# All block sums on VectorE, and a first pair that begins with products without sums

## The chip, the cores and the metric

The kernel runs on one core of one Trainium2 chip. The core has five engines, each with its own in-order queue: TensorE (PE) for matmuls, with PEld loading its weights beside it, VectorE (DVE), ScalarE (ACT), GpSimd (POOL) and SyncE (SP), which issues most of the DMA transfers. The metric is the device time of one execution in microseconds (us); the median of three runs counts.

## What is computed

One layer of a hybrid decoder on 1024 positions of width 1024: a feed-forward block, a mixer, a second feed-forward block, each behind a norm that a conditioning vector `c` scales and shifts. Cut to the part that the change touches (sh, sc and g come from `silu(c) @ w_ada + b_ada`):

```python
def swiglu(h, w_gate, w_up, w_down):
    return (jax.nn.silu(h @ w_gate) * (h @ w_up)) @ w_down

h = modulate(rmsnorm(x, norm_ffn1[l]), sh1, sc1)
x = x + 0.5 * g1[:, None, :] * swiglu(h, ffn1_w_gate[l], ffn1_w_up[l], ffn1_w_down[l])
h = modulate(rmsnorm(x, norm_mix[l]), sh2, sc2)
x = x + g2[:, None, :] * hybrid_mixer(h, ...)
h = modulate(rmsnorm(x, norm_ffn2[l]), sh3, sc3)
x = x + 0.5 * g3[:, None, :] * swiglu(h, ffn2_w_gate[l], ffn2_w_up[l], ffn2_w_down[l])
```

All is float32; the hidden width of each feed-forward block (FFN1, FFN2) is 2816, that is 22 tile columns of 128.

## The kernel before

**Split products.** Each float32 operand is split into a high part rounded to fp32r (`whi`, `bh`) and a low part, the difference (`wlo`, `bl`). A product is three passes on PE: high by high (line 167 in `mm3`), high weight by low input (line 168), low weight by high input (line 169). A weight tile's split (`parts`) is a cast on ACT (line 158) and a subtraction on DVE (line 159). The loaded weights (`raw`) have four slots, so have `whi` and `wlo`.

**Gate and up.** In each FFN the first two tile columns (the *first tiles*) are plain three-pass products. The other twenty are done in ten pairs. A pair is a 2x2 block product by a scheme of seven products instead of eight (`seven`, lines 384 to 431), once for gate and once for up, 168 matmuls of 128x512 in all. Its order is product 1, 2, 6, 5, 7, 4, 3. Products 1, 2 and 4 take blocks of the input as they are; 3, 5, 6 and 7 take sums of blocks, s4, s1, s2 and s3. Of the weights, products 1, 2 and 3 take loaded blocks, 6 and 5 the sums `ta`, 7 and 4 the sums `tb`.

**The sums.** `blocks` (lines 344 to 363) makes the input sums of an FFN once, behind its first tiles: 16 additions of high and low on POOL (line 354), 16 sums on DVE (lines 355 to 358), then a cast on ACT (line 360) and a subtraction on DVE (line 361) for each. `weight_blocks` (lines 365 to 382) makes four sums for each weight on POOL (line 372), 160 in both FFNs, and splits all seven parts. The weight sums stand in tiles `comb`.

**Around the pairs.** After each product a copy on ACT (line 398) keeps a partial result and additions on DVE (line 394) finish it; silu on ACT and the product of gate and up on DVE (line 486) follow, and POOL stores the result (line 446). In FFN1 `side_work` runs between the pairs: `ada_vec` computes nine slices of the conditioning (512 KB loads, additions on DVE in line 209), and `rope_tables` the position tables (some 46 small DVE operations). Here the scheduler of the tile framework sets the order on each engine; a few places are pinned.

**First tiles.** In FFN1 (`first_tiles`) the first half of the positions has been done during startup; the second half is scaled (line 303), shifted and cast on ACT (line 308) and its low part formed on DVE (line 312), step by step, then the first tiles' second half runs. `act` (line 449) makes silu and product of a tile column. In FFN2 `first_tiles2` does both halves. **Behind the pairs** `hidden` loads the results back as inputs of the down projection, and `down` (line 515) loads the down weights when it first needs them.

Of the kernel before, what the change touches and what calls it, by code (L numbers as in the profile page):

```python
# [15 lines left out]
ALU = mybir.AluOpType  # L16
# [43 lines left out]
ACT0 = (3, 6)  # L60
# [45 lines left out]
class Layer:  # L106
# [25 lines left out]
    def open_weights(self, nraw, nsplit, size):  # L132
        if self.wctx is not None:
            self.wctx.close()
        self.wctx = ExitStack()
        self.ctx.push(self.wctx)
        self.wts = self.wctx.enter_context(self.tc.tile_pool(name="wts", bufs=1, side="right", reuse_waits="tile"))
        self.wraw, self.wsplit, self.wsize = nraw, nsplit, size

# [174 lines left out]
    def ada_norm(self, xT, b, hh, hT, tp, spread=(), order=None, make=None):  # L314
# [3 lines left out]
        if make is not None:  # L318
            hT.append(make())
        for j in range(KT):  # L320
# [23 lines left out]
    def blocks(self, hT, s1, s2, s4, tp):  # L344

        nc = self.nc
        (h0, l0), (h1, l1) = hT
        s3 = (h1[:, 0:4], l1[:, 0:4])
        f = lambda x: x.bitcast(F32)
        for j in range(4):  # L350
            t = {}
            for name, (h, l), k in (("a21", hT[1], j), ("a22", hT[1], j + 4), ("a11", hT[0], j), ("a12", hT[0], j + 4)):
                t[name] = tp.tile([P, 512], F32, name="g", bufs=8)
                nc.gpsimd.tensor_tensor(out=t[name], in0=f(h[:, k]), in1=f(l[:, k]), op=ALU.add)
            nc.vector.tensor_tensor(out=t["a22"], in0=t["a21"], in1=t["a22"], op=ALU.add)
            nc.vector.tensor_tensor(out=t["a21"], in0=t["a11"], in1=t["a21"], op=ALU.subtract)
            nc.vector.tensor_tensor(out=t["a11"], in0=t["a22"], in1=t["a11"], op=ALU.subtract)
            nc.vector.tensor_tensor(out=t["a12"], in0=t["a12"], in1=t["a11"], op=ALU.subtract)
            for name, (hi, lo) in (("a11", s2), ("a22", s1), ("a12", s4), ("a21", s3)):
                nc.scalar.copy(out=hi[:, j], in_=t[name])  # L360
                nc.vector.tensor_tensor(out=lo[:, j], in0=t[name], in1=f(hi[:, j]), op=ALU.subtract)  # L361
        half = lambda p, i: (p[0][:, 4 * i:4 * i + 4], p[1][:, 4 * i:4 * i + 4])
        return {1: half(hT[0], 0), 2: half(hT[0], 1), 3: s4, 4: half(hT[1], 1), 5: s1, 6: s2, 7: s3}

    def weight_blocks(self, w, t):
# [4 lines left out]
        ta, tb = [self.wts.tile([P, 8, P], F32, name="comb", bufs=2) for _ in range(2)]  # L370
        b11, b21, b12, b22 = r1[:, 0:4], r1[:, 4:8], r2[:, 0:4], r2[:, 4:8]
        tt = lambda o, x, y, op: nc.gpsimd.tensor_tensor(out=o, in0=x, in1=y, op=op)  # L372
# [5 lines left out]
        for src, names in ((r1, (1, 2)), (ta, (6, 5)), (tb, (7, 4)), (b22, (3,))):  # L378
            hi, lo = self.parts(src, (4 * len(names), P))
            for i, n in enumerate(names):  # L380
                out[n] = [(hi[:, 4 * i + k], lo[:, 4 * i + k]) for k in range(4)]
        return out

    def seven(self, A, B, new):
# [5 lines left out]
        def product(n, out, first):  # L390
            self.mm3(out, B[n], self.krows(A[n]), first=first, skip=not first)
# [42 lines left out]
    def ffn(self, hT, sums, xd, wg, wu, wd, b, tp, side, begin, mid, quarters, ws):  # L434
# [13 lines left out]
        def act(ps, t, hh):  # L448
            s = self.tmp.tile([P, 512], F32, name="t")
            nc.scalar.activation(out=s, in_=ps[0], func=AF.Silu)  # L450
            a = tp.tile([P, 512], F32, name="g", bufs=8)
            nc.vector.tensor_tensor(out=a, in0=s, in1=ps[1], op=ALU.mult)
# [15 lines left out]
        begin(load, gateup_mm, act, gateup)  # L468
        A = self.blocks(hT, *sums(), tp)
# [45 lines left out]
        def down(c, o, hh, n, c0=0, w=512):  # L515
# [1208 lines left out]
```

## Time and profile before

| what | us |
|---|---|
| median of three runs (lowest, highest) | 2371.13 (2369.62, 2372.92) |
| the profiled execution | 2369.87 |
| its span on the core | 2368.1 |
| PE busy | 2200.5 |
| DVE busy | 1414.8 |
| ACT busy | 877.4 |
| POOL busy | 446.4 |

The profile is one execution; its span is what the engines took, the execution's own time has a little around it. Busy time is the sum of an engine's instructions. PE's is modelled, and a matmul's row is longer than the distance to the next one, so small stops show in the distance only. A line of waits says for whom an engine stood still (the producer that came last), how long in all and how often. FFN1's pairs lie between 107 and 580 us of the span, FFN2's between 1658 and 2085; the mixer is between them.

### The profile page before, as it was taken

How to read it: one execution, taken by the hardware profiler on the slowest of the kernel's cores; microseconds unless marked ns; L12 is line 12 of the kernel's file. 1: busy time of each engine (PE TensorE's matmuls, PEld its weight loads, DVE VectorE, ACT ScalarE, POOL GpSimd, SP SyncE). 2: the span in 40 equal slices, each digit the busy share in tenths (PEclk: the TensorE clock that was granted, in tenths of full speed). 3: DMA queues.
4: the chain of work that ended last, by engine and by line, in shares of the span. 5: the costliest groups of instructions: out<-in, count | busy, mean ns of one | idle time of the engine just before them, and what ended most of it. 6: DMA issues, size and time to landing. Idle time of an engine off the chain costs nothing. (4 is left out here: it accounts for less than half of the span.)

```text
span 2368.1 us, 27357 instructions
## 1 busy us (share of the span) xinstructions
PE 2200.5 (93%) x10431; PEld 1800.2 (76%) x10431; DVE 1414.8 (60%) x2151; ACT 877.4 (37%) x1409; POOL 446.4 (19%) x428
## 2 busy tenths in 40 slices
PE   5859999999999999999999999999599999989997
PEld 4647777777878778877778898887477777768787
DVE  7896775445333664456986888867744444443346
ACT  4232223333112433276534766623333333321133
POOL 4443223331000110000212011102533333200000
PEclk9879999999999999999999999999799999999999
DMA  8124655226233331245554000232022222252234
GB/s 290 37 91 162 195 188 167 81 80 222 62 107 103 108 119 45 64 127 155 188 187 134 16 19 22 90 134 85 22 85 76 85 76 85 76 205 80 98 111 138
DMA packets 113491, 261.36 MB, mean 110 GB/s; under 512 B 10208, under 2 KB 31072, under 8 KB 113360
## 3 DMA queue, kind: packets, MB, share of 16 engines
q1 hardware_dynamic: 97712, 214.85, 28.1%
q0 software_dynamic: 11088, 37.17, 4.3%
q10 hardware_dynamic: 4560, 7.60, 0.9%
q8 instruction: 82, 1.34, 0.2%
q14 instruction: 49, 0.40, 0.1%
HBM read 212.46 MB, written 47.12 MB: 110 GB/s over the span
## 5 line engine op out<-in xcount | busy, mean ns | idle before, releaser
L167 PE MATMUL dn<-bh,whi 128*128 128x512 f32 (+1 forms) x1104 | 426.7, 387 | 19.8 <-ACT whi L158 17.5
L169 PE MATMUL dn<-bh,wlo 128*128 128x512 f32 (+1 forms) x1104 | 425.7, 386 | 3.2 <-DVE wlo L159 1.6
L168 PE MATMUL dn<-bl,whi 128*128 128x512 f32 (+1 forms) x1104 | 425.6, 386 | 2.4 <-DVE bl L306 2.4
L158 ACT CAST whi<-raw 128x1024 fp32r<-128x1024 f32 (+4 forms) x230 | 205.7, 897 | 530.5 <-PE dn L168 253.9
L167 PE MATMUL mm<-bh,whi 128*128 128x512 f32 x880 | 349.6, 398 | 20.0 <-ACT whi L158 8.6
L169 PE MATMUL mm<-bh,wlo 128*128 128x512 f32 x880 | 345.7, 394 | 6.3 <-DVE wlo L159 5.7
L168 PE MATMUL mm<-bl,whi 128*128 128x512 f32 x880 | 344.3, 392 | 0.7 <-DVE bl L361 0.7
L159 DVE TENSOR_TENSOR wlo<-raw,whi 128x1024 fp32r<-128x1024 f32 (+3 forms) x219 | 249.3, 1138 | 128.5 <-ACT whi L158 126.5
L167 PEld LDWEIGHTS dn<-bh,whi 128*128 128x128 f32 x1104 | 211.1, 191 | 63.2 <-ACT whi L158 20.5
L169 PEld LDWEIGHTS dn<-bh,wlo 128*128 128x128 f32 x1104 | 210.9, 191 | 46.4 <-DVE wlo L159 3.9
L168 PEld LDWEIGHTS dn<-bl,whi 128*128 128x128 f32 x1104 | 210.9, 191 | 44.8 <-DVE bl L306 3.3
L159 DVE TENSOR_TENSOR wlo<-comb,whi 128x1024 fp32r<-128x1024 f32 x80 | 98.9, 1238 | 212.0 <-ACT whi L158 209.7
L524 DVE SCALAR_TENSOR_TENSOR x<-dn,gat,x 128x512 f32<-128x512 f32 (+1 forms) x104 | 73.7, 708 | 246.8 <-PE dn L169 246.8
L167 PEld LDWEIGHTS mm<-bh,whi 128*128 128x128 f32 x880 | 165.9, 189 | 60.2 <-DVE t L394 10.7
L169 PEld LDWEIGHTS mm<-bh,wlo 128*128 128x128 f32 x880 | 166.2, 189 | 47.2 <-DVE wlo L159 12.2
L168 PEld LDWEIGHTS mm<-bl,whi 128*128 128x128 f32 x880 | 166.5, 189 | 34.7 <-DVE bl L361 1.0
L158 ACT CAST whi<-comb 128x1024 fp32r<-128x1024 f32 x80 | 84.2, 1053 | 229.9 <-PE mm L168 208.3
L372 POOL TENSOR_TENSOR comb<-raw 128x512 f32<-128x512 f32 x80 | 108.5, 1360 | 263.7 <-DVE wlo L159 170.4
L167 PE MATMUL mm<-x,whi 128*128 128x512 f32 x280 | 112.6, 403 | 32.9 <-ACT g L398 22.1
L169 PE MATMUL mm<-x,wlo 128*128 128x512 f32 x280 | 112.7, 403 | 6.4 <-DVE wlo L159 5.1
L168 PE MATMUL mm<-x,whi 128*128 128x512 f32 x280 | 111.4, 398 | 1.9 <-DVE x L312 1.2
L446 POOL DMA_DIRECT2D a_d<-g x88 | 48.4, 550 | 301.4 <-DVE g L486 253.5
(337 smaller groups left out, 3821.2 us busy)
## 6 DMA issues: line engine op xcount, KB each, us to landing
raw<-w_ada SPq DMA_DIRECT2D x56, 512.0 KB, 4.1
raw<-wg SPq DMA_DIRECT2D x44, 512.0 KB, 3.6
raw<-wu SPq DMA_DIRECT2D x44, 512.0 KB, 3.5
a_d<-g POOLq DMA_DIRECT2D x88, 256.0 KB, 2.5
raw<-a_d SPq DMA_DIRECT2D x44, 512.0 KB, 4.2
raw<-wd SPq DMA_DIRECT2D x32, 512.0 KB, 4.6
raw<-win SPq DMA_DIRECT2D x31, 512.0 KB, 3.5
raw<-wd SPq DMA_DIRECT2D x40, 384.0 KB, 3.2
```

The lines of the kernel that those rows point to most:

```text
L158: self.made = nc.scalar.copy(out=hi, in_=r)
L159: (engine or nc.vector).tensor_tensor(out=lo, in0=r, in1=hi.bitcast(F32), op=ALU.subtract)
L167: nc.tensor.matmul(out=out, lhsT=ah, rhs=bh, start=first and i == 0, stop=False, skip_group_check=skip)
L168: nc.tensor.matmul(out=out, lhsT=ah, rhs=bl, start=False, stop=False, skip_group_check=skip)
L169: nc.tensor.matmul(out=out, lhsT=al, rhs=bh, start=False, stop=last and i == n - 1, skip_group_check=skip)
L372: tt = lambda o, x, y, op: nc.gpsimd.tensor_tensor(out=o, in0=x, in1=y, op=op)
L446: nc.gpsimd.dma_start(out=a_d[t, :, hh * 512:hh * 512 + 512], in_=a)
L524: nc.vector.scalar_tensor_tensor(out=xs, in0=ps[:, 0:w], scalar=self.gat[:, 8 * b + o:8 * b + o + 1], in1=xs, op0=ALU.mult, op1=ALU.add)
```

## The change

All block sums move from POOL to DVE, and the code around them is written in another order:

- `blocks` becomes `second_half`. It scales all eight steps of the second half first, then makes high, shifted value and low of each step, the shifted value on ACT and in place, in the order 0, 4, 1, 5, 2, 6, 3, 7. After the first tiles it makes the other sums, on DVE.
- `weight_blocks` makes its sums on DVE and splits a part only when a product asks for it (`get`).
- The first pair begins with products 1 and 2 of gate and of up. Then come 6, 5, 7 of gate, 6 of up, 4 and 3 of gate, 5 and 7 of up, and 4 and 3 of up in the next pair.
- In FFN1 the first eleven steps of the side work (the slice `ada_vec(2)` and the loads behind it) are issued behind the last block subtraction.
- `act` writes in place; `ACT0`, which put the first half's `act` between two steps, is gone. The first down weights are loaded ahead of the first hidden tiles; in FFN2 the stores of x (`x3_d`) come ahead of the first tiles. The tiles of a weights pool are declared when it is opened.

The diff, cut to its core:

```diff
-    def blocks(self, hT, s1, s2, s4, tp):
+    def second_half(self, x, r, b, hT, s2, rest, tp):
...
+        order = (0, 4, 1, 5, 2, 6, 3, 7)
+        t, u = {}, {}
+        for j in order:
+            t[j] = tp.tile([P, 512], F32, name="g", bufs=8)
+            nc.vector.scalar_tensor_tensor(out=t[j], in0=self.cols(x, j, 512, 512), scalar=self.scl[:, 8 * b + j:8 * b + j + 1],
+                                           in1=r, op0=ALU.mult, op1=ALU.mult)
+        s1, s4 = rest()
         s3 = (h1[:, 0:4], l1[:, 0:4])
-        f = lambda x: x.bitcast(F32)
+        for j in order:
+            shift = self.mod[:, 24 * b + j:24 * b + j + 1]
+            nc.scalar.activation(out=h1[:, j], in_=t[j], func=AF.Identity, bias=shift)
+            nc.scalar.activation(out=t[j], in_=t[j], func=AF.Identity, bias=shift)
+            nc.vector.tensor_tensor(out=l1[:, j], in0=t[j], in1=f(h1[:, j]), op=ALU.subtract)
+
+        yield None
...
+        def split(src, dst, j):
+            nc.scalar.copy(out=dst[0][:, j], in_=src)
+            self.made = tt(dst[1][:, j], src, f(dst[0][:, j]), ALU.subtract)
+
         for j in range(4):
-            t = {}
-            for name, (h, l), k in (("a21", hT[1], j), ("a22", hT[1], j + 4), ("a11", hT[0], j), ("a12", hT[0], j + 4)):
-                t[name] = tp.tile([P, 512], F32, name="g", bufs=8)
-                nc.gpsimd.tensor_tensor(out=t[name], in0=f(h[:, k]), in1=f(l[:, k]), op=ALU.add)
-            nc.vector.tensor_tensor(out=t["a22"], in0=t["a21"], in1=t["a22"], op=ALU.add)
...
+            whole(j)
+            tt(t[j + 4], t[j], t[j + 4], ALU.add)
+            tt(t[j], u[j], t[j], ALU.subtract)
+            tt(u[j], t[j + 4], u[j], ALU.subtract)
+            split(u[j], s2, j)
+            split(t[j + 4], s1, j)
+        for j in range(4):
+            split(t[j], s3, j)
+            whole(j + 4)
+            tt(u[j + 4], u[j + 4], u[j], ALU.subtract)
+            split(u[j + 4], s4, j)
...
     def weight_blocks(self, w, t):
...
-        tt = lambda o, x, y, op: nc.gpsimd.tensor_tensor(out=o, in0=x, in1=y, op=op)
+        tt = lambda o, x, y, op: nc.vector.tensor_tensor(out=o, in0=x, in1=y, op=op)
...
+        def get(n):
+            if n not in out:
+                src, names = next(x for x in ((r1, (1, 2)), (ta, (6, 5)), (tb, (7, 4)), (b22, (3,))) if n in x[1])
+                hi, lo = self.parts(src, (4 * len(names), P))
...
-        begin(load, gateup_mm, act, gateup)
-        A = self.blocks(hT, *sums(), tp)
+        A = begin(load, gateup_mm, act, gateup)
+        made = self.made.ins
...
-            for us in (g, up_units(t, res)):
+            u = up_units(t, res)
+            if t == 2:
+                self.weave(g[:2] + u[:2])
+                if side is not None:
+                    with self.tc.issue_after(made):
+                        for _ in range(11):
+                            next(side)
+                self.weave(g[2:5] + u[2:3] + g[5:] + u[3:5], [side])
+                held = u[5:]
+                continue
+            for us in (g, u):
...
+        weights(0, 0, 8)
         hidden(0, 0, 8)
```

In the changed code the matmul lines are 170 to 172, the weight cast and subtraction 161 and 162, the block sums 377, the weight sums 405, the additions 431, the product of gate and up 522, that of the first tiles 488.

PE at the end of the first pair's gate products 1 and 2 in FFN1, before (`bh_88` and `bl_89` are the input's first half, `x_670` holds sums):

```order
L168 MATMUL mm<-bl_89,whi 128x512
L167 MATMUL mm<-x_670,whi 128x512
L168 MATMUL mm<-x_670,whi 128x512
L169 MATMUL mm<-x_670,wlo 128x512
L167 MATMUL mm<-x_670,whi 128x512
L168 MATMUL mm<-x_670,whi 128x512
```

and now (`bh_92`, `bl_93` the same half, `s_522` the sum s2), at the end of the second of up:

```order
L172 MATMUL dn<-bh_92,wlo 128x512
L170 MATMUL dn<-bh_92,whi 128x512
L171 MATMUL dn<-bl_93,whi 128x512
L172 MATMUL dn<-bh_92,wlo 128x512
L170 MATMUL mm<-s_522,whi 128x512
L171 MATMUL mm<-s_522,whi 128x512
L172 MATMUL mm<-s_522,wlo 128x512
```

Where gate's product 2 ran straight into a product with sums, up's products 1 and 2 now stand before it.

DVE in FFN1's first pair before: the last first-tile products (line 452) and weight splits, then the block sums and subtractions (355 to 361), which wait for POOL:

```order
L159 TENSOR_TENSOR wlo<-raw,whi 128x1024
L452 TENSOR_TENSOR g<-t,dn 128x512
L159 TENSOR_TENSOR wlo<-comb,whi 128x1024 x2
L452 TENSOR_TENSOR g<-t,dn 128x512
L159 TENSOR_TENSOR wlo<-raw,whi 128x512
L355 TENSOR_TENSOR g<-g 128x512
L207 TENSOR_SCALAR t<-raw,cact 128x512
L356 TENSOR_TENSOR g<-g 128x512
```

and now: after the last first-tile product (line 488) come the block sums of line 377, of which the list shows the last ones, and only then the low half of `comb`, that is of ta, for product 6:

```order
L377 TENSOR_TENSOR x_539<-t,x_539 128x512
L377 TENSOR_TENSOR t<-t 128x512
L377 TENSOR_TENSOR t<-bh_92,bl_93 128x512
L431 TENSOR_TENSOR g<-g,dn 128x512
L377 TENSOR_TENSOR x_539<-t,x_539 128x512
L377 TENSOR_TENSOR t<-t 128x512
L431 TENSOR_TENSOR t<-t,dn 128x512
L162 TENSOR_TENSOR wlo<-comb,whi 128x1024
L377 TENSOR_TENSOR x_539<-t,x_539 128x512
L405 TENSOR_TENSOR comb<-raw 128x512
```

The rows between are of the same kind: from the product of line 488 to that subtraction there are 32 operations of 128x512, two of them additions of line 431. In FFN2's first pair the same count stands ahead of the low half of tb, which product 7 needs.

DVE in a late pair of FFN2 before, about the end of gate's product 2 (line 394 is an addition that waits for PE, here `dn` holds product 2):

```order
L394 TENSOR_TENSOR t<-t,mm 128x512
L159 TENSOR_TENSOR wlo<-raw,whi 128x512
L486 TENSOR_TENSOR g<-g,t 128x512
L394 TENSOR_TENSOR g<-g,dn 128x512
L159 TENSOR_TENSOR wlo<-raw,whi 128x1024
L159 TENSOR_TENSOR wlo<-comb,whi 128x1024
```

and now:

```order
L431 TENSOR_TENSOR t<-t,mm 128x512
L162 TENSOR_TENSOR wlo<-raw,whi 128x1024
L522 TENSOR_TENSOR g<-g,t 128x512
L431 TENSOR_TENSOR g<-g,dn 128x512
L162 TENSOR_TENSOR wlo<-raw,whi 128x512
L162 TENSOR_TENSOR wlo<-comb,whi 128x1024
```

The low half of up's loaded blocks (`wlo<-raw,whi 128x1024`), which stood behind the product of line 486 and the addition of gate's product 2, now stands ahead of both. The weight sums of line 405 follow a few rows on.

## Rows read from the trace of the kernel before

**Rows 1.** The page's part 1: busy us (share of the span) xinstructions, by engine.

```profile
PE 2200.5 (93%) x10431; PEld 1800.2 (76%) x10431; DVE 1414.8 (60%) x2151; ACT 877.4 (37%) x1409; POOL 446.4 (19%) x428
```

**Rows 2.** What PE waited for, 100 to 160 us: total us, times, longest.

```profile
PE mm L167 <- ACT g L398: 21.9, 1, 21.9
PE mm L167 <- ACT whi L158: 8.6, 1, 8.6
```

**Rows 3.** The same, 1650 to 1705 us.

```profile
PE mm L167 <- ACT g L398: 17.8, 1, 17.8
PE mm L167 <- ACT whi L158: 7.7, 1, 7.7
```

**Rows 4.** Stretches: length, busy us (xinstructions) by engine, PEclk, DMA share, GB/s.

```profile
145.00:155.00 10.00, 8.77 (x23) 5.80 (x22) 9.94 (x17) 3.69 (x6) 0.55 (x1) 0.67 0.26 80
...
1691.00:1701.00 10.00, 8.60 (x21) 5.85 (x22) 7.64 (x12) 4.24 (x7) 0.00 (x0) 0.67 0.15 52
...
2094.00:2098.00 4.00, 3.96 (x10) 2.73 (x11) 2.20 (x2) 1.04 (x1) 0.00 (x0) 0.59 0.89 283
```

**Rows 5.** Timeline, first pair: start, us, engine, operation [idle before <-releaser].

```profile
127.33 1.71 POOL L372 TENSOR_TENSOR comb<-raw 128x512 f32<-128x512 f32 x1
...
126.16 1.75 DVE L361 TENSOR_TENSOR s<-g,s 128x512 fp32r<-128x512 f32 x1
...
146.01 0.68 DVE L356 TENSOR_TENSOR g<-g 128x512 f32<-128x512 f32 x1
146.62 0.68 DVE L361 TENSOR_TENSOR x<-g,x 128x512 fp32r<-128x512 f32 x1
...
143.64 0.58 ACT L398 COPY g<-mm 128x512 f32<-128x512 f32 x1
```

**Rows 6.** PE's timeline in FFN2's first pair: single matmuls, six between these two.

```profile
1702.28 0.40 PE L167 MATMUL mm<-bh,whi 128*128 128x512 f32 x1
...
1703.87 0.39 PE L168 MATMUL mm<-bl,whi 128*128 128x512 f32 x1
```

**Rows 7.** Timeline: DVE before the first pair, PE's first matmul of either first pair.

```profile
69.58 3.43 DVE L842 TENSOR_TENSOR ada<-ada 128x512 f32<-128x512 f32 x2
...
83.17 2.08 DVE L303 SCALAR_TENSOR_TENSOR t<-x,scl,rs 128x512 f32<-128x512 f32 x3 [4.45 <-ACT rs L279]
...
104.21 1.22 DVE L159 TENSOR_TENSOR wlo<-raw,whi 128x1024 fp32r<-128x1024 f32 x1
...
106.98 0.39 PE L167 MATMUL mm<-bh,whi 128*128 128x512 f32 x1
...
1657.71 0.39 PE L167 MATMUL mm<-x,whi 128*128 128x512 f32 x1
```

**Rows 8.** The chain that ended last, FFN2's pairs: start, us, what.

```profile
1816.78 0.68 DVE g L394
...
1856.35 0.68 DVE g L394
```

**Rows 9.** PE's waits, 1705 to 2080 us, and 2080 to 2110 us.

```profile
PE mm L169 <- DVE wlo L159: 4.7, 9, 1.7
...
PE dn L167 <- ACT whi L158: 6.5, 2, 4.1
```

**Rows 10.** A stretch of FFN1's pairs beside the side work.

```profile
300.00:350.00 50.00, 44.31 (x194) 34.95 (x193) 34.20 (x46) 13.15 (x19) 14.19 (x12) 0.97 0.55 182
```

**Rows 11.** Operations, 160 to 400 us: xcount, busy us, mean ns, idle before, releasers.

```profile
L209 DVE SCALAR_TENSOR_TENSOR t<-raw,cact,t 128x512 f32<-128x512 f32 x92 | 74.2, 806 | 15.0 <-DMA raw<-w_ada 12.9
...
L486 DVE TENSOR_TENSOR g<-g,t 128x512 f32<-128x512 f32 x15 | 15.2, 1011 | 0.2
...
L372 POOL TENSOR_TENSOR comb<-raw 128x512 f32<-128x512 f32 x22 | 31.4, 1439 | 64.4 <-DMA raw<-wg 51.5 <-issue 4.3 <-DMA raw<-wu 3.7
```

**Rows 12.** Lines 394 and 486 in FFN2: ns min/median/max, first and last start.

```profile
L394 DVE TENSOR_TENSOR t<-t,mm x18: 686/688/689, 1732.9 to 2082.3; 128x512 f32<-128x512 f32 x18
...
L486 DVE TENSOR_TENSOR g<-g,t x27: 677/692/1782, 1734.4 to 2083.0; 128x512 f32<-128x512 f32 x27
```

More of the change, by code (lines that the diff above doesn't have):

```diff
@@ L138, in open_weights @@
         self.wraw, self.wsplit, self.wsize = nraw, nsplit, size
+        for name, dt, bufs in (("whi", F32R, nsplit), ("wlo", F32R, nsplit), ("comb", F32, 2), ("raw", F32, nraw)):
+            if name != "comb" or nraw == 4:
+                self.wts.tile([P, size], dt, name=name, bufs=bufs)
     def raw(self, src, shape):
@@ new lines, in second_half, with whole, tt @@
+        yield None
+        def whole(j):
+            u[j] = self.tmp.tile([P, 512], F32, name="t")
+            tt(u[j], f(h0[:, j]), f(l0[:, j]), ALU.add)
+        def tt(o, x, y, op):
+            return nc.vector.tensor_tensor(out=o, in0=x, in1=y, op=op)
+        def split(src, dst, j):
+            nc.scalar.copy(out=dst[0][:, j], in_=src)
+            self.made = tt(dst[1][:, j], src, f(dst[0][:, j]), ALU.subtract)
+        for j in range(4):
+            whole(j)
[4 more added lines that the diff above has]
+            split(t[j + 4], s1, j)
@@ L390, in product @@
         def product(n, out, first):
-            self.mm3(out, B[n], self.krows(A[n]), first=first, skip=not first)
+            self.mm3(out, B(n), self.krows(A[n]), first=first, skip=not first)
         def add(sb, bank):
@@ L448, in act @@
         def act(ps, t, hh):
[L449 to L452, printed above, removed]
+            a = self.tmp.tile([P, 512], F32, name="t")
+            nc.scalar.activation(out=a, in_=ps[0], func=AF.Silu)
+            nc.vector.tensor_tensor(out=a, in0=a, in1=ps[1], op=ALU.mult)
             put(a, t, hh)
@@ L696, in run @@
             sq = []
-            def sums2():
-                for hh in range(2):
-                    nc.gpsimd.dma_start(out=x3_d[:, :, hh * 512:hh * 512 + 512], in_=xT[hh])
-                t = [self.main.tile([P, KT, 512], F32R, name=n) for n in ("bh1", "bl1")]
-                t.append(tp.tile([P, KT, 512], F32R, name="s4", bufs=1))
-                return [(x[:, 0:4], x[:, 4:8]) for x in t]
             def quarters(xT, c0):
@@ L883, in go @@
             load(1)
+            s2 = tp.tile([P, KT, 512], F32R, name="s2", bufs=1)
+            for hh in range(2):
+                self.nc.gpsimd.dma_start(out=x_d[:, :, hh * 512:hh * 512 + 512], in_=xT[hh])
             self.weave(gateup(0, 0) + gateup(1, 0), [self.norm1, self.norm1], drain=True)
+            blocks = self.second_half(xT, self.r1, 2, hT, (s2[:, 0:4], s2[:, 4:8]), rest, tp)
+            next(blocks)
             self.weave(gateup(0, 1) + gateup(1, 1))
+            return next(blocks)
         return go
```

68 lines of the change are left out of this document (34 added, 34 removed).

## The prediction

> **What bounds the kernel now.** I read the page's busy shares first, then what TensorE (PE) waited for around each FFN's first pair, then the chain that ended last in the other pairs. PE is busy 93% of the span, VectorE (DVE) 60%, GpSimd (POOL) 19% [rows 1], so time can be won only where PE stands still. It does so twice for long. Between FFN1's first two tile columns and its first pair it waits 8.6 and 21.9 us [rows 2]; in FFN2 7.7 and 17.8 us [rows 3]. After each, PE having stood still, the granted clock is 0.67 of full over the next 10 us, part at 1.2 and part at 2.4 GHz, with 23 and 21 matmuls in them [rows 4]; at full clock seven pitches take 1.59 us, 0.227 each [rows 6], so these stretches lose another 10 - 23 x 0.227 = 4.8 us and 10 - 21 x 0.227 = 5.2 us. Zone 1 costs 8.6 + 21.9 + 4.8 = 35.3 us, zone 2 30.7 us: 66 us, all that the first pairs can give.
>
> The cause is in the timeline. The waits name ACT copies (the longer one L398, which began at 143.64 behind the casts of the block sums on ACT), but those stand in line behind DVE, and DVE behind POOL. Beside a POOL sum of 1.71 us, a DVE subtraction of 128x512 takes 1.75 us; once POOL is through, the same takes 0.68 and starts every 0.60 [rows 5].
>
> **The change, part by part.** The sum is made against the profiled execution (2369.87 us); the median of the three runs is 2371.13, 1.3 us more, which I add at the end.
>
> *Start of the first tiles, FFN1.* POOL's four weight sums at 66 to 72 us go. The two L842 additions beside them took 3.43 us instead of some 1.3 [rows 7], so DVE is about 2 us earlier there; the same four sums now stand on DVE (4 x 0.60 = 2.4 us), mostly in gaps of the short root chain. I take 2 us earlier, bounds 0 and 3. Against that, all eight scalings now come before the first subtraction. One takes 0.67 (2.08 for three, pitch 0.67 [rows 7]), so eight take 5.3 us where three took 2.0: the second matmul, which needs the first low half, comes 3.3 us later. A wait of 4.1 us [rows 9] left 10 matmuls in 4 us at clock 0.59 [rows 4], a loss of 4 - 2.3 = 1.7 us; I charge 1.2 since it is not sure to fall here. The first tiles end 2.5 us later (bounds 0 and 5): before, product 1 begins at 107.0 [rows 7], now at 109.5. The position (rope) work on DVE, which ends before the first weight subtraction at 104.2 [rows 7], is not pinned; the order leaves it there, where PE is busy with the first tiles and hides it.
>
> *First pair, FFN1.* PE goes on with products 1 and 2 of gate and of up: 48 matmuls, 10.9 us, to 120.4. The next, product 6, needs the low half of weight sum ta. On DVE it stands behind the second first-tile product (0.7 us after the tiles end, plus its silu on ACT 0.6, so from about 110.8) and 32 operations of 128x512, nearly all of them block sums. At 0.60 these take 19.2 us, to 130.0; the subtraction itself 1.2 (the 128x1024 row of [rows 7]): 131.2. PE waits 10.8 us, and I add 2.0 for the clock behind it (1.7 behind 4.1 us, 4.8 behind 21.9). So zone 1 costs 2.5 + 10.8 + 2.0 = 15.3 instead of 35.3: **20.0 us gained**. Bounds: with the bare 0.60 and no clock loss 25; if each of the 32 takes 0.9 (a cast of 0.6 between sum and subtraction uncovered in half of them), 10.
>
> *First pair, FFN2.* The four weight sums fall in waits of DVE. The first tiles lose 3.3 us by the same eight scalings, less 0.7 for the weight subtraction no longer beside POOL: 2.6, so that product 1 begins at 1657.7 [rows 7] + 2.6 = 1660.3 and the 48 matmuls last to 1671.2. Here ta's half stands ahead of the block sums on DVE, which start behind the first tiles' last product (1661.6); the low halves that product 6 needs are there by 1661.6 + 19 x 0.60 = 1673.0, about PE's last step of it; product 5 ends at 1676.7. Product 7's weight half is behind 32 operations: 1661.6 + 0.6 + 19.2 + 1.2 = 1682.6, a wait of 5.9. Up's product 6 waits 1.4 for its own (three sums, a product and a subtraction further down DVE's line, 4.1 us, less 12 matmuls, 2.7), the clock takes 1.7, kept copies that come late on ACT 0.8. Cost 2.6 + 5.9 + 1.4 + 1.7 + 0.8 = 12.4 instead of 30.7: **18.3 us gained**, bounds 10 and 24. The stores of x3_d are issued earlier on POOL; they run beside the first tiles and nobody waits for them.
>
> *The other pairs.* In FFN2 the add after product 2 recurs every 39.57 us [rows 8]; 168 matmuls at 0.227 are 38.1. Of the missing 1.4 us, 0.5 is PE's recorded wait for wlo (4.7 us in 9 [rows 9]); as a matmul's row outlasts its pitch by 0.17, a short stop shows only in part. DVE is late there since line 486, which has two SBUF inputs, takes 1782 instead of 677 ns beside POOL [rows 12], and since the split of the next weights stands behind the adds. Both go: POOL is empty, and the order has that subtraction ahead of the adds. I take 1.0 us from 9 pairs (**9 us**) and 0.8 from the five pairs of FFN1 behind the side work (**4 us**); bounds 0 and 1.4 each, so 0 and 20 together.
>
> *FFN1's pairs beside the side work.* DVE takes the sums over, 8 per pair; 43 of them (22 of the form in [rows 11]) stood on POOL from 160 to 400 us, 43 x 0.60 = 26 us. It loses the slowdown: 92 adds of line 209 at 806 instead of about 680 ns (11.6 us) and 15 of line 486 at 1011 instead of 677 (5.0) [rows 11, 12], with the wlo groups some 22 us. DVE's load of 34.2 in 50 us [rows 10] stays within 1 us of that, so I take 0, bounds -10 and +10. Here a rule bears on the size. Line 394, with one operand in PSUM, is never slowed (686 to 689 ns), line 486 with both in SBUF is [rows 12]. The Trainium skill, SBUF — State Buffer (Who interferes with whom), says that a VectorE operation with two SBUF inputs and a GpSimd operation that reads SBUF block each other to the end, and one with a single SBUF input is untouched: the trace agrees. By that rule a POOL sum could cost DVE up to its whole 1.44 us, an estimate of 62 us freed for 26 added, and this term would be -10 rather than 0; by the rows' means it is 22 for 26.
>
> *Into the down projection.* Down weights are loaded ahead of the hidden tiles. PE's two waits of 6.5 us there [rows 9] lose the first (4.1, and its 1.7 of slow clock); the second weight tile still queues behind the hidden loads on SP, and I let that wait grow by 2.8: **3 us**, bounds 0 and 5. In FFN1 that load was in front already: nothing.
>
> Edits with one answer: `act` writing in place and the tiles declared beforehand save buffers, no work (0). The pinned gate sums (ada_vec(2)) leave DVE during the first pair and are made up behind it, ten loads ahead of pair 2's weights on SP; charged with the side work above.
>
> Sum: 20.0 + 18.3 + 9 + 4 + 0 + 3 = 54 us; 2369.9 - 54 + 1.3 = **2317 us**.
>
> **The rivals.**
> *A. DVE's line of 32 sums runs at 0.9, not 0.60.* Place: both first pairs, sum, cast on ACT, subtraction. Price 32 x 0.3 = 9.6 us each, 19 together: 2336. Against: at 146 us the old code ran sum after subtraction at 0.60 with the casts between [rows 5]. For: each sum of a block still needs its cast on ACT before the subtraction, and the last three steps of a chain have little else to fill the time.
> *B. More goes.* The side-work stretch gains its 10 us and the first pairs' new waits shrink by 4 each: 2317 - 18 = 2299.
> *C. Slower than before: weight loads now block DVE.* POOL waited 51.5 us for wg in the side-work stretch [rows 11]; only stores and later sums stood behind it. Now these sums stand on DVE, in order, with PE's subtractions and adds behind. If all of it became PE's wait, with a fifth more for the slow clock behind it (4.8 behind 21.9 [rows 2, 4]), 51.5 + 10.3 = 62 us: 2317 + 62 = 2379. It decides from 54 us on, nearly the whole; against it, DVE reaches these sums later than an empty POOL did, and DVE's own waits for w_ada (12.9 us [rows 11]) already run in that time. The Trainium skill, Perfetto Trace Analysis (Optimizing Scalar/DVE Operations), would move work off a saturated VectorE, even to GpSimd, the reverse of this change; DVE is busy 68% of that stretch [rows 10], not saturated.
> *D. It doesn't do what it says:* the sums come quicker but another input of product 6 (up's weights, a kept copy) holds PE as long. Then the two gaps keep all but a few us and only the pairs gain, lost again in the side work: 2369. Against: the order has all of these ahead of the sums.
>
> **How the numbers follow.** Forecast 0.54 (its own range 2304 to 2330), A 0.20, B 0.14, C 0.07, D 0.05. The range reaches through A with 6 us more and down to B: 2298 to 2342; outside lie C, D and some 0.06 of the tails. About 0.2% (4.7 us) can be told from no change here. Faster is the forecast, A, B and a fifth of D (0.89), same 0.04, slower C (0.07).
>
> **What would show it.** POOL's busy time falls from 446 us to about 446 - 160 x 1.4 - 32 x 1.7, some 170; DVE two-input 128x512 rows stand at 0.68 everywhere. PE's gaps: about 11 us near 120, about 6 us near 1655 (that zone now some 24 us sooner), none of 18 or 22. The add of FFN2's pairs recurs every 38.5 us. Wrong would be: a wait of DVE for raw<-wg of over 5 us with PE idle behind it (C); gaps of 16 to 20 us (A); a gap whose releaser is no DVE subtraction (D).

## The result and the profile after

| what | before | after |
|---|---|---|
| median, us (lowest to highest of four runs each) | 2371.97 (2369.62 to 2372.92) | 2300.06 (2296.36 to 2302.97) |
| the profiled execution, us | 2369.87 | 2300.07 |
| its span, us | 2368.1 | 2297.9 |

The ratio is 0.9697, 95% interval 0.9681 to 0.9714: about 72 us faster. Forecast were 2317 us with a range of 2298 to 2342. The time is inside the range, near its fast end; the gain is 17 us more than the sum of the terms, and rival B (2299) is nearest.

Busy time by engine after (the page's part 1), to be read against [rows 1]:

```profile
PE 2182.9 (95%) x10431; PEld 1795.4 (78%) x10431; DVE 1432.3 (62%) x2327; ACT 884.2 (38%) x1425; POOL 174.0 (8%) x236
```

POOL fell to 174 us (some 170 were forecast). DVE carries 176 operations more and is busy 17.5 us longer; at 0.60 the added ones alone would be 106 us. The rest is the slowdown beside POOL that went.

What PE waited for in the first pairs after, from 75 to 135 us (FFN1) and then from 1590 to 1705 us (FFN2); they answer to [rows 2] and [rows 3]. Columns: engine, tile and line, releaser, total us, times, longest.

```profile
PE mm L172 <- DVE wlo L162: 10.1, 1, 10.1
PE dn L171 <- DVE bl L368: 3.2, 1, 3.2
PE dn L170 <- ACT bh L366: 2.4, 1, 2.4
```

```profile
PE mm L172 <- DVE wlo L162: 4.3, 1, 4.3
PE mm L171 <- DVE bl L368: 1.6, 2, 1.0
PE mm L170 <- ACT g L435: 1.0, 1, 1.0
```

The four long waits (8.6 and 21.9, 7.7 and 17.8) became two, of 10.1 and 4.3 us, both for a low half of weights, as the forecast had them (10.8 and 5.9).

What stands behind the first of them, DVE's timeline after (start, us, engine, operation), to be read against [rows 5]:

```profile
110.54 0.68 DVE L488 TENSOR_TENSOR t<-t,dn 128x512 f32<-128x512 f32 x1
111.14 0.68 DVE L377 TENSOR_TENSOR g<-t,g 128x512 f32<-128x512 f32 x1
111.74 0.68 DVE L377 TENSOR_TENSOR t<-bh,bl 128x512 f32<-128x512 f32 x1
...
129.80 0.67 DVE L431 TENSOR_TENSOR t<-t,dn 128x512 f32<-128x512 f32 x1
130.40 1.21 DVE L162 TENSOR_TENSOR wlo<-comb,whi 128x1024 fp32r<-128x1024 f32 x1
```

From 111.14 to 130.40 there are exactly the 32 operations that were counted, 0.602 us apart, with no idle time between them. Rival A (0.9 each) is out.

PE's timeline at the same wait: the last matmul ahead of it, the first two behind it, and the last slow one with its neighbours.

```profile
121.19 0.39 PE L171 MATMUL mm<-s,whi 128*128 128x512 f32 x1
131.67 0.80 PE L172 MATMUL mm<-s,wlo 128*128 128x512 f32 x1 [10.09 <-DVE wlo L162]
132.26 0.63 PE L170 MATMUL mm<-s,whi 128*128 128x512 f32 x1
...
134.82 0.63 PE L170 MATMUL mm<-s,whi 128*128 128x512 f32 x1
135.25 0.55 PE L171 MATMUL mm<-s,whi 128*128 128x512 f32 x1
135.63 0.39 PE L172 MATMUL mm<-s,wlo 128*128 128x512 f32 x1
```

Behind the wait the matmuls are 0.43 instead of 0.227 us apart until 135.6: the granted clock is 0.51 there, the lower of PE's two levels (1.2 GHz). Nine of them cost about 2 us, as charged.

**Where the 70 us of span came from.** In each pair the addition `t<-t,dn` (line 394, now 431) runs once, so the same addition can be found in every trace. Its start before less its start after is the gain up to that point; a column of the table is the difference between two such points. Point 2 is this addition of the second pair of FFN1 (215.0 us before), and so on; the last stretch runs to the end of the span.

| stretch | forecast | measured |
|---|---|---|
| FFN1's first pair, to pair 2 | 20.0 | 15.9 |
| pairs 2 to 6, beside the side work | 0 | **12.3** |
| pairs 6 to 10 of FFN1 | 4 | 4.1 |
| down projection, mixer and norm, to FFN2's product 1 | 0 | 2.0 |
| FFN2's product 1 to its pair 2 | 18.3 | **25.0** |
| FFN2's pairs 2 to 10 | 9 | 8.8 |
| last pair and down projection | 3 | 2.1 |
| sum | 54 | 70.2 |

### The profile page after: what moved, and what is told of

It is laid out like the page before. It is cut to its first block, busy times and chain, and to the rows that moved or that the text cites. A ratio compares the mean times of both kernels' runs of the same rounds, so it can differ in the third digit from the quotient of the medians.

```text
span 2297.9 us, 27236 instructions
## 1 busy us (share of the span) xinstructions
PE 2182.9 (95%) x10431; PEld 1795.4 (78%) x10431; DVE 1432.3 (62%) x2327; ACT 884.2 (38%) x1425; POOL 174.0 (8%) x236
## 4 chain that ended last, share of the span: by engine, by line
PE 75%; DVE 11%; DMA 6%; issue 5%; ACT 2%; POOL 1%; SPq 0%; DVEq 0%; POOLq 0%; ACTq 0%
PE mm L170 12%; PE mm L171 12%; PE mm L172 12%; PE dn L171 11%; PE dn L172 11%; PE dn L170 11%; DMA raw<-w_ada 2%; PE dn L1645 1%; DVE wlo L162 1%; DVE acc L777 1%; DVE t L212 1%; DVE t L377 1%; DVE comb L405 1%; DMA M<-ac_d 1%; DMA raw<-wg 1%
## 5 line engine op out<-in xcount | busy, mean ns | idle before, releaser
L162 DVE TENSOR_TENSOR wlo<-raw,whi 128x1024 fp32r<-128x1024 f32 (+3 forms) x219 | 227.0, 1038 | 133.5 <-ACT whi L161 131.3
L171 PE MATMUL mm<-x,whi 128*128 128x512 f32 x280 | 109.5, 392 | 0.0
L483 POOL DMA_DIRECT2D a_d<-g x80 | 43.2, 540 | 791.8 <-DVE g L522 750.9
L556 ACT CAST bh<-raw 128x1024 fp32r<-128x1024 f32 x44 | 43.5, 1048 | 131.3 <-PE dn L172 114.8
```

The costliest lines, as they stand in the source:

```text
L162: (engine or nc.vector).tensor_tensor(out=lo, in0=r, in1=hi.bitcast(F32), op=ALU.subtract)
L171: nc.tensor.matmul(out=out, lhsT=ah, rhs=bl, start=False, stop=False, skip_group_check=skip)
L483: nc.gpsimd.dma_start(out=a_d[t, :, hh * 512:hh * 512 + 512], in_=a)
L556: nc.scalar.copy(out=hi, in_=r)
```

## The experiments

Two theories stood against each other for the larger part that nobody had counted. *Contention*: POOL's sums slow DVE's two-input operations wherever they run side by side. *Lateness and order*: a sum on POOL (1.44 us against 0.60) is late for the product that needs it, and the new order brings the urgent things forward. The same points as above, as gains over before in us, for the runs that bear on it:

| run | to pair 2 | pairs 2 to 6 | pairs 6 to 10 | to FFN2's pair 2 | FFN2's pairs | end | sum |
|---|---|---|---|---|---|---|---|
| the changed kernel | 15.9 | 12.3 | 4.1 | 27.0 | 8.8 | 2.1 | 70.2 |
| weight sums back on POOL | 8.0 | -10.7 | 3.2 | 21.5 | 4.9 | 1.6 | 28.4 |
| before, weight sums on DVE | 9.2 | 15.9 | 3.2 | 1.2 | 8.1 | 0.7 | 38.2 |
| before, block sums on DVE | 6.6 | -0.7 | 0.1 | 10.2 | 0 | 0.8 | 17.0 |
| before, both on DVE | 8.4 | 14.1 | 3.6 | 10.9 | 8.8 | 1.5 | 47.1 |
| odd tile, POOL as in the changed kernel | 16.0 | 11.6 | 1.0 | 9.6 | 2.7 | -4.6 | 36.3 |
| odd tile and idle POOL work | 15.4 | -2.6 | -1.5 | 5.8 | -2.2 | -3.6 | 11.3 |
| 1600-byte tile and idle POOL work | 14.1 | -0.3 | 0.4 | 19.8 | 1.5 | -0.5 | 35.0 |

These are spans of one profiled execution each. The times below are medians of four, and single executions of a kernel lie up to 10 us apart; the row with both on DVE shows the slowest of its four. The start is one cause: in the changed kernel's trace the first scaling of FFN1's second half begins at 81.2 us, in seven of the runs below at 76.9 to 78.6, with the same instructions in the same order up to there. So first columns differ by some 2 to 4 us by the start alone.

### Weight sums back on POOL

```diff
-        tt = lambda o, x, y, op: nc.vector.tensor_tensor(out=o, in0=x, in1=y, op=op)
+        tt = lambda o, x, y, op: nc.gpsimd.tensor_tensor(out=o, in0=x, in1=y, op=op)
```

> The changed kernel, with the 160 weight sums back on POOL and nothing else. Contention theory (what the pairs gained is DVE freed of POOL's sums): the pairs lose their 0.9 us each again (9 in FFN2, 5 in FFN1, 13 us), the side-work stretch its 9 to 12 us, and the first pairs some 2 each: about 2300 + 27 = 2327 us, the add after product 2 in FFN2 recurring every 39.4 us. Order theory (the gain is that the split of the next weights now stands ahead of the adds): the pairs keep 38.6 us and the time is 2300 to 2306.

Measured: 2342.23 us, ratio to before 0.9877 (0.9862 to 0.9892). Both theories were too low. This one line is worth 42 us of the 72, over half of it (23 us) in the stretch beside the side work, for which the forecast had nothing. There the new order with sums on POOL is even 10.7 us slower than before.

### The weight sums alone, in the kernel before

```diff
-        tt = lambda o, x, y, op: nc.gpsimd.tensor_tensor(out=o, in0=x, in1=y, op=op)
+        tt = lambda o, x, y, op: nc.vector.tensor_tensor(out=o, in0=x, in1=y, op=op)
```

> The kernel before, with the 160 weight sums on DVE; the input's block sums stay as they were. Contention theory: the pairs fall to 38.6 us (13 us), the side-work stretch gains 9 to 12, the first pairs 2 or 3 each as their four weight sums no longer share POOL with the input's sums: about 2372 - 28 = 2344 us. Order theory: the split of the next weights stays behind the adds, so the pairs stay near 39.5 us, and the side work pays 5 us of DVE time a pair: 2365 to 2385.

Measured: 2329.37 us, 0.9822 (0.9805 to 0.9838): 42 us from the other side too, more than either theory had, though all code stands in its old order. The first pairs' long waits hardly move (30.5 to 28.7 us in FFN1); here those of FFN1 in this run, 100 to 160 us:

```profile
PE mm L167 <- ACT g L398: 17.3, 2, 16.5
PE mm L167 <- ACT whi L158: 11.4, 1, 11.4
```

Most of the gain lies in the pairs from the second on, where nothing waits for the block sums: 27 of the 38 us of span. Some 9 come ahead of FFN1's pair 2.

### The block sums alone, in the kernel before

```diff
-                nc.gpsimd.tensor_tensor(out=t[name], in0=f(h[:, k]), in1=f(l[:, k]), op=ALU.add)
+                nc.vector.tensor_tensor(out=t[name], in0=f(h[:, k]), in1=f(l[:, k]), op=ALU.add)
```

> The kernel before, with the 16 additions of high and low of the input (line 354) on DVE in each FFN; the weight sums stay on POOL. 48 operations of 0.60 us are 29 us in DVE's line where POOL's 16 additions of 1.7 us alone took 27 and held DVE's 32 at 1.75 us. From the first tiles' end at 109 us the sums should be through near 140 instead of 150 us, so 8 to 10 us less in each FFN: about 2354 us. If it is the placing and the order of products that made the gain, not the engine, the time stays within 4 us of 2372.

Measured: 2357.35 us, 0.9939 (0.9922 to 0.9956): 14 us, near the 18 expected of the engine and far from none. By span nearly all of it falls in the two first pairs (6.6 and 10.2) and nothing between, which is a check on the table's method.

### Both moves without the new order

The two edits above in one kernel, all code in its old order.

> The kernel before with both moves and nothing else: 160 weight sums and 16 block sums on VectorE, all code in its old order, POOL left with stores and conditioning. Alone the moves gave 42 us and 15 us against the kernel before. If they add up, 2372 - 57 = about 2313 to 2316, and the new order (first pair woven, split on demand, scalings first, stores of x earlier) is worth the other 13 to 16 us. If the moves are everything, as the unwoven first pair (2304) suggests, 2300 to 2305. In the first pairs some 36 VectorE operations of 0.60 us stand ahead of the last input sum of product 6, 22 us, of which 24 matmuls cover 5.5: a wait of TensorE of about 16 us should stand there, where the changed kernel has 10.1 and 4.3.

Measured: 2315.94 us, 0.9753 (0.9732 to 0.9774). The moves add up (42 + 14 = 56; measured 58), so the new order is worth the rest: 13 us by the two ratios, 16 by the medians. The waits of the first pairs show where, here in FFN1 (100 to 160 us) and then in FFN2 (1590 to 1705 us):

```profile
PE mm L167 <- ACT g L398: 17.4, 2, 16.7
```

```profile
PE mm L167 <- ACT g L398: 16.4, 1, 16.4
```

About 16 us were worked out from 36 operations ahead of product 6's last sum, less 24 matmuls that cover 5.5. With the sums s2 and s1 made first and the first products of up put ahead it is 10.1 and 4.3.

### The first pair in its old order of products

```diff
-                self.weave(g[:2] + u[:2])
...
-                self.weave(g[2:5] + u[2:3] + g[5:] + u[3:5], [side])
-                held = u[5:]
-                continue
```

> The changed kernel, with the first pair in the old order of products (gate alone, then up), the pinned side work as it is. If the block sums set when product 6 may begin, PE's wait before it grows by the 24 matmuls of up that no longer cover it, 5.4 us in each FFN: about 2311 us, with a wait near 15 us at 131 us in FFN1. If something else than the sums holds product 6, the wait keeps its 10 us and the time stays at 2300.

Measured: 2304.29 us, 0.9713 (0.9697 to 0.9729), 4 us behind the changed kernel by medians and ratios, with intervals that overlap. (Its span is within 1 us of it, but in a trace that began 4.0 us ahead at the first scaling.) The products that need no sums, which the change puts ahead, gain that much at most, and the wait neither grew to 15 us nor stayed at 10. The waits from 100 to 160 us show why:

```profile
PE dn L191 <- DVE t L212: 3.4, 2, 2.4
PE mm L172 <- DVE wlo L162: 2.9, 1, 2.9
PE mm L171 <- DVE s L377: 1.7, 3, 0.7
```

Here the scheduler put ta's low half ahead of the block sums, since product 6 asks for it sooner, and PE follows the sums one by one. In the changed kernel the same half stands behind 32 sums, and the 24 matmuls of up (5.5 us) only cover what that adds. So of the 13 to 16 us for the new order some 4 belong to the order of the products. The rest belongs to the other edits, the order of the sums, the split on demand and the smaller ones; no run parts these.

### POOL kept busy with work that nobody needs

```diff
+        self.extra = self.const.tile([P, NCONST], F32, name="extra")
...
+                for _ in range(2):
+                    nc.gpsimd.tensor_tensor(out=self.extra, in0=g[k][:, 0:NCONST], in1=self.kc, op=ALU.add)
```

> The changed kernel with 160 additions on POOL that nobody needs: two of 128x401 behind each store of a pair's result (one operand the result, one a constant, the output never read), the rows of all other engines in the same order. E1 put the needed sums back on POOL and lost 42 us. If DVE's slowdown beside POOL makes that loss, this kernel loses most of it too: 2330 to 2345 us, with DVE's adds of line 212 back near 820 ns. If the loss is that PE waits for a sum which POOL delivers late (four sums of 1.4 us in a row instead of 0.60, behind other work in POOL's line), nothing waits for these and it stays at 2300 to 2308.

Measured: 2359.54 us, 0.9952 (0.9935 to 0.9969), slower than both theories allow, also where the added work doesn't run: from FFN1's last pair to FFN2's first it took 19 us longer. PE's 128x512 matmuls were 0.233 instead of 0.227 us apart in every stretch looked at. Either POOL's work or the added tile (1604 bytes on each partition) had to be the cause, and the next two runs part them.

### The same with a tile of 1600 bytes, and the odd tile alone

```diff
+        self.extra = self.const.tile([P, 400], F32, name="extra")
...
+                for _ in range(2):
+                    nc.gpsimd.tensor_tensor(out=self.extra, in0=g[k][:, 0:400], in1=self.kc[:, 0:400], op=ALU.add)
```

> The changed kernel with 160 additions of 128x400 on GpSimd that nobody reads, as in the run with idle GpSimd work, but into a tile of 1600 instead of 1604 bytes per partition. The orders on TensorE, VectorE and ScalarE are those of the changed kernel, and no sum is late. If the earlier run lost mainly to slower dense matmuls (0.233 instead of 0.227 us apart) that came with the odd tile, the pitch is back at 0.227 here, and what stays is the contention for SBUF alone: the earlier run lost 14.8 us in the stretch beside the side work, of which 170 us of TensorE at 2.7% are 4.6; that leaves about 10 us there and 3 to 4 us in the other pairs: 2312 to 2318. If GpSimd's work itself slows the matmuls, 2350 to 2362 with a pitch of 0.233. If contention is worth nothing and only the lateness of GpSimd's sums cost time, 2300 to 2305.

```diff
+        self.extra = self.const.tile([P, NCONST], F32, name="extra")
+        nc.gpsimd.tensor_copy(out=self.extra, in_=self.kc)
```

> The changed kernel with the odd tile of 1604 bytes per partition and one copy into it at the start, and no other GpSimd work. The orders on TensorE, VectorE and ScalarE are those of the changed kernel. If the odd tile moves what lies behind it to addresses at which matmuls read their operands more slowly, the pitch is 0.233 and the time about 2300 + 0.006 x some 9600 matmuls at full pitch, 2340 to 2357. If the slow pitch came from GpSimd's work, 2300 within 3.

Measured: 2338.42 us, 0.9849 (0.9828 to 0.9869), for the work with the 1600-byte tile; 2333.13 us, 0.9823 (0.9800 to 0.9846), for the odd tile without work. So the tile alone costs 33 us by the medians, 30 by the ratios, less than the 40 to 57 expected: beside the side work, where PE waits anyway, it costs 0.7. The run with the work is outside all three of its ranges, since its matmuls aren't back at 0.227. PE in FFN1's down projection shows it, in the changed kernel, with 1600 bytes, and with 1604 (in each, 15 matmuls from the first row to the second):

```profile
701.65 0.39 PE L172 MATMUL dn<-bh,wlo 128*128 128x512 f32 x1
...
705.05 0.39 PE L172 MATMUL dn<-bh,wlo 128*128 128x512 f32 x1
```

```profile
701.95 0.39 PE L173 MATMUL dn<-bh,wlo 128*128 128x512 f32 x1
...
705.39 0.39 PE L173 MATMUL dn<-bh,wlo 128*128 128x512 f32 x1
```

```profile
701.69 0.39 PE L174 MATMUL dn<-bh,wlo 128*128 128x512 f32 x1
...
705.19 0.39 PE L174 MATMUL dn<-bh,wlo 128*128 128x512 f32 x1
```

That is 3.40, 3.44 and 3.50 us, a pitch of 0.227, 0.229 and 0.233. The 1600-byte run is thus still clouded by some 1% of PE's time. The clean pair is the two runs with the odd tile: the same tiles and the same order on PE, DVE and ACT, one with 160 idle additions on POOL and one without. Their busy times, first with the work and then without:

```profile
PE 2228.6 (95%) x10431; PEld 1794.2 (76%) x10431; DVE 1507.5 (64%) x2327; ACT 882.2 (37%) x1425; POOL 374.4 (16%) x396
```

```profile
PE 2221.2 (95%) x10431; PEld 1794.6 (77%) x10431; DVE 1434.4 (62%) x2327; ACT 883.8 (38%) x1425; POOL 173.9 (7%) x237
```

DVE is busy 73 us longer with the same instructions, 0.46 us for each POOL addition of 1.25 us. Its additions hold the pair's results longer, too, but only one wait of DVE, 1.0 us, is put down to that. Which operations pay is seen in FFN2's pairs, 1700 to 2040 us (ns min/median/max), in the run with the work, weight sums with two inputs in SBUF and additions with one in PSUM. One of each kind ran beside a POOL addition there: the weight sum took 1894 ns, the addition 674.

```profile
L406 DVE TENSOR_TENSOR comb<-raw,comb x17: 678/683/1894, 1716.3 to 2036.6; 128x512 f32<-128x512 f32 x17
...
L432 DVE TENSOR_TENSOR t<-t,mm x18: 674/682/689, 1706.3 to 2037.2; 128x512 f32<-128x512 f32 x18
```

The Trainium skill, SBUF — State Buffer (Who interferes with whom), names the first kind as the one that contends with a GpSimd operation reading SBUF, and the second as free of it; these rows agree, and so does the kernel before, where 59 of the 120 additions of line 394 ran beside a POOL sum and none took over 689 ns.

By span the idle work costs 25 us (2356.8 against 2331.8), by the two ratios 31, and no sum is late for it. In the stretch beside the side work it is 14 us (11.6 + 2.6), of the 23 that the weight sums on POOL cost there; in the other pairs 7.4 (2.5 + 4.9), more than they cost there (0.9 + 3.9). The run with 1600 bytes agrees: it is 12.6 us behind the changed kernel beside the side work, and the odd tile alone 0.7. So contention by itself is shown, and if the weight sums contend as the idle additions do, it is 25 to 31 of the 42 us. Some 11 to 17 are left for sums that come late and for POOL's longer time on them (1.39 us each); no run parts these.

### Weight halves ahead of the later block sums

```diff
+        self.early()
         for j in range(4):
             split(t[j], s3, j)
+        self.early2()
+        for j in range(4):
             whole(j + 4)
...
+        def early():
+            for w in (wg, wu):
+                pre[id(w)] = self.weight_blocks(w, 2)
+                pre[id(w)](1)
+            pre[id(wg)](6)
...
+        def early2():
+            pre[id(wg)](7)
+            pre[id(wu)](6)
```

The pin on the first side work stays: it begins at 133.6 us, behind the last block subtraction at 132.4.

> The changed kernel, with the splits of the first pair's weights pulled ahead in DVE's line: the half of ta (product 6) behind the sums s1 and s2, those of tb (product 7) and of up's ta behind s3, all ahead of s4. If DVE's line of 32 operations is what PE's 10.1 us wait in FFN1 and its 4.3 us wait in FFN2 stand for, product 6 begins some 8 us sooner in FFN1 and the waits fall under 3 us: 2300 - 10 = 2290 us, or 2288 to 2294. If the wait only moves to the next product that needs a sum (s3, then s4), it stays within 3 us of 2300.

Measured: 2294.50 us, 0.9669 (0.9652 to 0.9686), half a us outside the range. The waits of 10.1 and 4.3 are gone, 100 to 160 us and then 1590 to 1705:

```profile
PE mm L170 <- ACT t L438: 3.6, 1, 3.6
PE mm L170 <- DVE t L434: 1.6, 1, 1.6
```

```profile
PE mm L170 <- ACT t L438: 3.6, 2, 2.9
```

Their releaser was thus the sums ahead of the halves, as the forecast said. Of 14.4 us of wait some 6 became time, and that is barely clear of the noise, since the two ratios' intervals touch. Kept copies and additions come late in their place.

### Scaling step by step again

```diff
+        s1, s4 = rest()
+        s3 = (h1[:, 0:4], l1[:, 0:4])
         for j in order:
             t[j] = tp.tile([P, 512], F32, name="g", bufs=8)
             nc.vector.scalar_tensor_tensor(out=t[j], in0=self.cols(x, j, 512, 512), scalar=self.scl[:, 8 * b + j:8 * b + j + 1],
                                            in1=r, op0=ALU.mult, op1=ALU.mult)
-        s1, s4 = rest()
-        s3 = (h1[:, 0:4], l1[:, 0:4])
-        for j in order:
```

> The changed kernel, with each step's scaling next to its low half again instead of all eight scalings first. If the eight scalings delay FFN1's first tiles (PE waits 3.2 us behind four matmuls, then nine matmuls at half clock), this wait falls to about 1 us and the first tiles end 2 to 4 us sooner; the sums on DVE do not begin sooner by that much, so 2297 to 2300 us. If DVE's line is the bound from the start to product 6, only the wait moves and the time is 2300 within 2.

Measured: 2290.81 us, 0.9661 (0.9646 to 0.9675), 9 us better than the changed kernel. Its waits from 75 to 135 us:

```profile
PE mm L172 <- DVE wlo L162: 10.1, 1, 10.1
...
PE dn L171 <- DVE bl L367: 0.4, 1, 0.4
```

The wait of 3.2 us for the first low half is 0.4, and, against my expectation, none of it comes back in the wait for product 6: the 32 sums follow the first tiles wherever these end, so the whole of DVE's line moved up with them. At pair 2 this run is 8.0 us ahead of the changed kernel. Of these, 2.9 were there at the first scaling (78.3 against 81.2 us), ahead of all that the edit touches. Scaling all steps first is a loss in the change; the 5 us that remain are what the forecast charged (3.3 us and up to 1.7 for the clock).

### Both of these edits together

> The changed kernel with both edits that helped alone: the halves of the first pair's weight sums pulled ahead of the later block sums, and the eight scalings back inside the steps of the second half. Alone they gave 2294.5 and 2290.8. If the two gains are apart (a shorter wait of TensorE in the first pairs, and an earlier start of the whole VectorE line), 2300 - 5.5 - 9 = about 2285 to 2287. If the second takes what the first would have hidden, 2290 to 2294.

Measured: 2293.89 us, 0.9661 (0.9643 to 0.9680), not different from either edit alone. The gains don't add; which of them is lost was not settled. No kernel's median is below the step-by-step kernel's 2290.81, 9 us faster than the changed kernel.

### Down weights loaded late

```diff
-        weights(0, 0, 8)
         hidden(0, 0, 8)
```

> The changed kernel with the first down weights loaded behind the hidden tiles again. The term of the sum for it was 3 us: about 2303 us, with PE's first wait for a down weight back at 4 us. If the load was hidden anyway, 2300 within 1.

Measured: 2298.66 us, 0.9694 (0.9679 to 0.9708): no difference by the times, where 3 us were expected. PE's waits as FFN2's down projection begins (2000 to 2060 us), in the changed kernel and then without the early load:

```profile
PE dn L170 <- ACT whi L161: 6.7, 1, 6.7
```

```profile
PE dn L170 <- ACT whi L161: 6.1, 2, 4.5
...
PE dn L172 <- DVE wlo L162: 1.0, 1, 1.0
```

With the early load, waits of 7.1 us in all became one of 6.7, so the waits alone give little. But from the last pair's addition to the end of the span this run takes 296.3 us and the changed kernel 293.3. This run had come to that point 5.2 us ahead, 2.7 of it at the first scaling, where the edit changes nothing. So the load may well be worth its 3 us; the times can't tell.

## Why the prediction was right, and where it was not

**Right: the cause and the new waits.** POOL's sums held DVE, and DVE held PE. The longer wait came out as counted: 32 operations at 0.60 to 131.2 us forecast, 131.67 measured. The two other-pair terms were right to a few tenths (4.1 for 4, 8.8 for 9). The addition of FFN2's pairs recurs every 38.66 us (forecast 38.5; [rows 8] 39.57):

```profile
1734.73 0.68 DVE L431 TENSOR_TENSOR t<-t,dn 128x512 f32<-128x512 f32 x1
...
1773.39 0.68 DVE L431 TENSOR_TENSOR t<-t,dn 128x512 f32<-128x512 f32 x1
```

What the forecast of these pairs says of its causes is half right. It takes both the slowed products and the place of the split as causes ("both go"); the sums moved in the old order give 0.9 to 1.0 a pair, the new order with sums on POOL 0.5 to 0.6, and the two together no more than the first.

**The term that was mis-sized: the side-work stretch, 0 for 12.3 us.** The step counted DVE's load, 26 us of sums added and 22 us of slowdown gone, found them equal, and took no gain. The count was about right, but it didn't set the time. Pairs 2 to 6 (length, busy us by engine as in [rows 4], clock, DMA) in the trace of before, with the weight sums alone on DVE, after, and with the odd tile and idle POOL work:

```profile
215.02:400.53 185.51, 171.99 (x764) 137.11 (x763) 129.68 (x170) 52.94 (x74) 59.16 (x52) 0.98 0.57 184
```

```profile
205.85:375.47 169.62, 166.08 (x761) 134.70 (x760) 137.25 (x206) 52.94 (x74) 8.64 (x16) 1.00 0.61 202
```

```profile
199.15:372.37 173.22, 165.68 (x753) 133.38 (x752) 133.63 (x200) 54.31 (x74) 8.63 (x16) 1.00 0.57 189
```

```profile
199.58:387.64 188.06, 174.32 (x753) 136.78 (x752) 154.34 (x199) 53.83 (x74) 51.22 (x48) 0.97 0.53 174
```

The first two hold the same side work, 80 operations on the conditioning's loads each: with the sums DVE is busy 7.6 us longer, and the stretch is 15.9 us shorter. (The changed kernel has only 74 of these operations there, as seven more of them stand ahead of its pair 2; part of its 12.3 us is that.) So DVE's sum didn't set the time, at 70% busy before and 81% with the sums. What did are the single operations that PE waits behind; its recorded waits in the stretch fall from 13.2 us to 3.4, and to 7.5 in the changed kernel. They stop PE for a few tenths to some two us at a time (PE's waits of 200 to 380 us, before):

```profile
PE mm L167 <- DVE t L394: 4.3, 3, 2.0
PE mm L169 <- DVE wlo L159: 2.9, 3, 1.5
PE dn L188 <- DVE t L209: 2.6, 2, 2.3
```

The additions of line 394 aren't slowed themselves [rows 12] but come late in DVE's line; what made each late was not followed. What POOL's additions alone do is seen in the two runs with the odd tile, whose order is the same. The longest waits there, 200 to 380 us, with the idle work and without:

```profile
PE mm L173 <- DVE wlo L163: 7.1, 4, 2.4
```

```profile
PE dn L193 <- DVE t L214: 2.4, 3, 1.2
```

With the stops the granted clock went (0.98 before and 0.97 with idle work, against 1.00). A sum added on DVE mostly fills time in which nobody waits; a subtraction that POOL slows, or an addition that comes late, is in front of a matmul. The two can have the same length and not the same price. The gain of 10 that the rule's full block would have given was nearer the time, but not for its reason: the measured slowdown of 0.46 us for each POOL operation is no more than the rows' means had it (22 us for 43, 0.51). So it was the price of a slowed operation, not its size, that was wrong.

**Under-sized: FFN2's first pair, 18.3 for 25.0.** The 2.6 us charged for its first tiles fall ahead of product 1, in the row above it. There product 1 began 34.3 us earlier than before and the second half's norm (ACT's copy `rs`) 36.2, so the first tiles did lose 1.9; but the norm came sooner than forecast, and why stays open. Behind product 1 the wait was 4.3 instead of 5.9, and up's product 6 didn't wait (1.4). The clock cost about 2 and the kept copies 1.0, near what was charged. That makes some 23 of the 25.

**Over-sized: FFN1's first pair, 20.0 for 15.9.** Product 1 began at 110.1 (forecast 109.5), the wait was 10.1 (10.8), the clock's price as charged. These give 20 again; the missing 4 us are lost between there and the addition of pair 2. Seven more operations of the side work stand ahead of that point than before (39 for 32), and PE's short waits behind them and behind additions come to 6.8 us from 132 us on (before, 4.3 behind the long wait). That this is the price was not tried by itself.

**The down projection, 3 for some 2.** The run without the early load took 3.0 us longer there by its trace, as charged; by its median nothing shows.

**The rivals.** B was right in size; of its two parts the side stretch came as it has it (10), the shorter waits only by 0.7 and 1.6. A fell with DVE's 0.602. C fell: DVE's weight sums hardly wait for loads (200 to 380 us, after; busy us, mean ns, idle before and its releasers):

```profile
L405 DVE TENSOR_TENSOR comb<-raw 128x512 f32<-128x512 f32 x18 | 12.0, 687 | 3.5 <-DMA raw<-wg 1.8 <-DMA raw<-wu 1.7
```

where POOL had waited 51.5 us [rows 11]. The Trainium skill's advice that was quoted for the reverse move, Perfetto Trace Analysis (Optimizing Scalar/DVE Operations), speaks of a saturated VectorE, and adds that between VectorE and GpSimd it might not help. The runs show what it costs when VectorE isn't: 42 us for 160 sums on GpSimd, at 60% VectorE busy. D fell with the releasers.

## What to carry to other kernels

When work moves off an engine that disturbs another, don't set the added busy time against the slowdown that goes: ask which operations stand right in front of the bounding engine and come late by the disturbance: each of these stops it, while added work in the gaps can cost nothing. Order the operations of a long in-order line by when their consumer needs them; reordering the consumer to cover the line gained some 4 us here. When an experiment adds a tile, run the tile alone too.

## What the runs showed of the hardware

A tile of 1604 bytes on each partition, written once and used by nobody, set the program's 128x512 matmuls 0.233 instead of 0.227 us apart, from the first tiles to the last projection and at full granted clock, and cost 30 to 33 us; with one of 1600 bytes they were 0.229 apart. The kernel with both edits above ran on the same chip as the odd tile alone and has 0.227, so it isn't the chip. Idle POOL work beside the odd tile changed nothing of it (0.233 too). That the tile moves the addresses of the matmuls' operands behind it is the likely cause, but no run shows it.
